# Attention's first two query blocks as one unit, and output rows turned with one PSUM bank at a time

## The chip, the cores and the metric

The kernel runs on one core of one Trainium2 chip. The metric is the device time of one execution in microseconds (us): lower is better. The kernel before takes 851.34 us, the median of three runs (850.49, 851.34, 851.52).

## What is computed

One layer of a hybrid encoder over 576 token columns: 512 of a prompt and 64 of a later chunk (the "sample"), model width 1024. One combined input projection feeds three groups of heads: a gated delta rule, a differential attention and a pooling mixer. Their outputs are concatenated, mapped back by `w_out`, added to the input, and a convolutional feed-forward network follows. The change touches the differential attention alone: 4 heads, each with two softmax maps of 64-dimensional keys, values of 128 dimensions, a block-causal mask and a norm for every head:

```python
def one_block(args):                      # prompt: blocks of 128 queries
    qi, bi = args
    q_chunk = (bi * Q_BLOCK + jnp.arange(Q_BLOCK)) // CHUNK
    mask = k_chunk[None, :] <= q_chunk[:, None]
    s = jnp.einsum('bqhmd,bkhmd->bhmqk', qi, k) * scale     # m: two maps
    s = jnp.where(mask, s, NEG_INF)
    p = jax.nn.softmax(s, axis=-1)
    w = p[:, :, 0] - lam * p[:, :, 1]
    return jnp.einsum('bhqk,bkhe->bqhe', w, v)
...
o_b = rmsnorm(o_b, b_norm) * (1.0 - lam_init)
```

Query block j (0 to 3) of the prompt sees key blocks 0 to j, so its two maps are 128 x 128(j+1).

## The kernel before

**Two streams on TensorE.** The large products (`gemm`, all through the helper `mm` at L85) form one long stream that `drive(projections())` walks. Every weight is split into a high and a low half (`w_hi`, `w_lo`) and so is every activation, and a product is three pairs of matmuls, 128 x 256 and 128 x 320 columns each, 576 in sum. Everything else (delta rule, attention, pooling) is written as generators that are put on a clock made of planned TensorE nanoseconds: `spawn(gen, delay)` starts one that many planned ns later, `yield N` puts its next piece N planned ns later, and `advance` issues what is due between two pairs of the stream. TensorE's order is the order in which this program issues matmuls; it is fixed at build time. The other engines' programs follow from it, and each runs its own in order.

**Banks.** Side work shares one pool of four PSUM banks (`psm`, tile name `m`, taken by `bank()`); the stream's results have two larger tiles of their own (`psg`, name `g`). In a row of the trace `m` is therefore a bank of the side work and `g` a result of the stream.

**One head of attention** (`attention()`, four heads one after the other). (1) `value_rows` turns the values with five transposes. (2) `scores_sample` fills two banks for the sample rows, and ScalarE takes the exponentials (L967, L968); `values_sample` needs one bank. (3) For j = 3, 2, 1, 0: `scores(a, j)` fills two banks with the maps; VectorE masks (L1005), takes maxima (L1006) and scales them (L1007); ScalarE takes the exponentials of both maps (L1010), which lets go of the banks; VectorE combines the maps into `p` (L1013 to L1016). Later `values(a, j)` takes a bank, transposes `p` into it (L1024, in the trace the helper's L89), ScalarE copies it out (L1026), the value matmuls write into the same bank, and VectorE copies the result into `oatt` (L1031); ScalarE sums its squares (L1033). At most three such units are in flight (`flight`). (4) When all five units of the head are done and the pooling groups too, `attn_out` computes the norm: VectorE L1040 to L1042, a reciprocal square root on GpSimd (L267), five scalings of `oatt` (L1047). After `yield 3500` it takes **two** banks at once, transposes the four prompt chunks into one and the sample chunk into the other, and ScalarE (L1055) and VectorE (L1056) write the high and low half of this head's rows of `mixed` (tile `wide`), 512 columns and then 64.

The attention of heads 1 to 3 overlaps the `w_out` products, whose order is the delta rule's and the pooling's inputs first, attention's last. Beside the attention VectorE also works for the stream: the low half of the weights (L175), of the pooling groups (L1149), the addition of the residual (L1159) and the low half of an early half-weight (L1095 in `own_weight`).

## Time and profile before

| | us |
|---|---|
| median of three runs | 851.34 |
| the profiled execution | 850.96 |
| its span, first to last instruction | 849.1 |
| TensorE busy in the span | 829.5 (98%) |
| VectorE busy | 536.0 (63%) |
| ScalarE busy | 359.9 (42%) |
| GpSimd busy | 109.5 (13%) |

1.9 us of the profiled execution lie outside its span. The attention runs from about 268 to about 400 us of the span. In the rows further down, a timeline row is: start, length in us, engine, line and operation, the tile written and the tiles read, shapes, how many instructions were joined (x), and in brackets how long the engine had been idle before it and who ended that idle time. Matmuls overlap at their ends, so the length of a joined row is longer than the distance from its start to the next row's start where nothing waits.

### The profile page before, as it was taken

Reading aid. Unit: us, or ns where it says so; the run is one execution under the profiler, and the core shown is the slowest. Engines: PE = TensorE matmul, PEld = TensorE weight load, DVE = VectorE, ACT = ScalarE, POOL = GpSimd, SP = SyncE. Lnnn points to the kernel's source line nnn. Section 1 sums busy time; section 2 is a strip of 40 time slices with the busy share of each in tenths; the row PEclk is TensorE's granted clock in tenths of the full one; section 3 lists DMA queues with packets and bytes.
Section 4 is the critical chain, followed back from the end, with each engine's and each line's share of the span. In section 5 each row is a group of like instructions: output and inputs, shape, how many; then the busy total and the mean of one; then the engine's idle time right before and its main releaser. Section 6 shows DMA issues by size and latency. Waiting matters only on the chain.

```text
span 849.1 us, 15939 instructions
## 1 busy us (share of the span) xinstructions
PE 829.5 (98%) x6342; PEld 803.9 (95%) x6342; DVE 536.0 (63%) x1203; ACT 359.9 (42%) x798; POOL 109.5 (13%) x166
## 2 busy tenths in 40 slices
PE   9989999999999999999999999999999999999996
PEld 8989999999999877789999999999999999999996
DVE  6798867881348667765767777776776773223423
ACT  7366661163444644543544444444434432222322
POOL 3132211220002000000011121121211210000001
PEclk9999999999999999999999999999999999999999
DMA  6242223242204323326622222222222223323313
GB/s 247 76 125 81 62 72 101 96 117 81 77 32 142 107 80 120 98 77 227 226 75 97 78 75 100 76 78 96 76 84 92 75 74 107 103 87 97 113 58 112
DMA packets 39032, 84.83 MB, mean 100 GB/s; under 512 B 9386, under 2 KB 14526, under 8 KB 38958
## 3 DMA queue, kind: packets, MB, share of 16 engines
q1 hardware_dynamic: 38014, 82.57, 30.1%
q10 hardware_dynamic: 944, 1.25, 0.4%
q8 instruction: 50, 0.82, 0.4%
q14 instruction: 24, 0.20, 0.1%
HBM read 72.98 MB, written 10.82 MB: 99 GB/s over the span
## 4 chain that ended last, share of the span: by engine, by line
PE 89%; DVE 4%; DMA 2%; ACT 2%; issue 1%; SPq 0%; POOLq 0%; POOL 0%; DVEq 0%; ACTq 0%
PE g L85 75%; PE m L85 11%; PE m L89 3%; DMA w_raw<-in_ffn_down_dram 1%; ACT w_hi L174 1%; DVE w_lo L175 1%; DMA x<-in_xT_dram 1%; DVE tmp L890 0%; DVE kq L596 0%; DMA w_raw<-in_w_out_dram 0%; ACT wide L348 0%; DVE oatt L1047 0%; DVE kq L601 0%; DVE p L1016 0%; DVE tmp L578 0%
## 5 line engine op out<-in xcount | busy, mean ns | idle before, releaser
L85 PE MATMUL g<-wide,w_hi 128*128 128x256 f32 x1472 | 265.6, 301 | 0.3
L85 PE MATMUL g<-t,w_hi 128*128 128x256 f32 (+1 forms) x1408 | 242.9, 294 | 0.0
L85 PEld LDWEIGHTS g<-wide,w_hi 128*128 128x128 f32 x1472 | 222.3, 190 | 2.9 <-DVE wide L349 0.6
L85 PEld LDWEIGHTS g<-t,w_hi 128*128 128x128 f32 x1408 | 210.2, 188 | 0.0
L174 ACT CAST w_hi<-w_raw 128x1024 fp32r<-128x1024 f32 (+2 forms) x109 | 110.9, 1017 | 172.8 <-PE g L85 161.8
L85 PE MATMUL g<-wide,w_lo 128*128 128x256 f32 x736 | 160.9, 300 | 0.5 <-DVE w_lo L175 0.5
L175 DVE TENSOR_TENSOR w_lo<-w_raw,w_hi 128x1024 fp32r<-128x1024 f32 (+2 forms) x109 | 128.2, 1176 | 49.9 <-ACT w_hi L174 48.9
L85 PE MATMUL g<-t,w_lo 128*128 128x256 f32 x704 | 150.2, 295 | 0.0
L85 PEld LDWEIGHTS g<-wide,w_lo 128*128 128x128 f32 x736 | 123.7, 190 | 2.5 <-issue 1.1
L85 PEld LDWEIGHTS g<-t,w_lo 128*128 128x128 f32 x704 | 117.4, 188 | 0.1
L1298 DVE SCALAR_TENSOR_TENSOR c<-u,par,c 128x511 f32<-128x511 f32 (+3 forms) x176 | 79.0, 512 | 2.5 <-ACT c L1294 2.5
L1301 POOL COPY fout<-u 128x4 f32<-128x4 f32 x44 | 51.2, 1163 | 223.1 <-DVE u L1292 223.1
L1292 DVE TENSOR_TENSOR u<-g,rstd 128x576 f32<-128x576 f32 x44 | 33.3, 758 | 59.7 <-PE g L85 58.2
L85 PE MATMUL g<-w,w_hi 128*128 128x256 f32 (+1 forms) x280 | 48.4, 295 | 0.0
L85 PEld LDWEIGHTS g<-w,w_hi 128*128 128x128 f32 x280 | 42.0, 188 | 0.0
L1294 ACT ACTIVATE c<-u,par 128x576 f32<-128x576 f32 x44 | 38.4, 873 | 4.6 <-DVE u L1292 1.8
L1318 ACT ACTIVATE s<-c 128x576 f32<-128x576 f32 x22 | 15.1, 688 | 45.8 <-DVE c L1300 45.8
L267 POOL TENSOR_TENSOR osc<-sso,mhalf 128x5 f32<-128x5 f32 x8 | 9.4, 1183 | 182.7 <-DVE sso L1042 77.9
L85 PE MATMUL g<-w,w_lo 128*128 128x256 f32 (+1 forms) x140 | 29.9, 294 | 0.0
L1203 ACT ACTIVATE junk<-m 128x128 f32<-128x128 f32 (+1 forms) x38 | 10.3, 274 | 40.2 <-PE m L89 32.2
L85 PE MATMUL g<-kq,w_hi 128*128 128x256 f32 (+1 forms) x128 | 25.0, 304 | 0.0
L1204 DVE TENSOR_TENSOR t<-m,nf 128x128 f32<-128x128 f32 (+1 forms) x38 | 10.6, 289 | 21.9 <-ACT junk L1203 21.9
(325 smaller groups left out, 1019.8 us busy)
## 6 DMA issues: line engine op xcount, KB each, us to landing
w_raw<-in_ffn_up_dram SPq DMA_DIRECT2D x44, 512.0 KB, 3.2
w_raw<-in_w_in_dram SPq DMA_DIRECT2D x30, 512.0 KB, 3.2
w_raw<-in_ffn_down_dram SPq DMA_DIRECT2D x16, 512.0 KB, 3.6
w_raw<-in_w_out_dram SPq DMA_DIRECT2D x8, 512.0 KB, 3.9
w_raw<-in_ffn_down_dram SPq DMA_DIRECT2D x8, 384.0 KB, 3.2
xr<-in_xT_dram SPq DMA_DIRECT2D x8, 288.0 KB, 3.2
x_d<-xr SPq DMA_DIRECT2D x8, 288.0 KB, 2.1
w<-x_d SPq DMA_DIRECT2D x8, 288.0 KB, 5.2
```

What stands on the lines that cost most here:

```text
L85: ordered(nc.tensor.matmul(out, lhsT=lhsT, rhs=rhs, start=start, stop=stop), n / 2.4 if rhs.dtype == F32R else max(54, n / 0.6))
L89: ordered(nc.tensor.transpose(out=out, in_=in_, identity=identity), 107)
L174: nc.scalar.copy(hi[:, :kt], raw)
L175: last_split[0] = nc.vector.tensor_sub(lo[:, :kt], raw, hi[:, :kt].bitcast(F32)).ins
L267: nc.gpsimd.tensor_tensor(out, x, epst[:x.shape[0], :x.shape[1]], op=ALU.pow)
L1203: nc.scalar.activation(junk[:n], src, AF.Square, scale=D ** -0.5, accum_out=op["part"][:n, c, m:m + 1])
L1204: nc.vector.tensor_mul(op["yt"][c][m // 4][:n, (m % 4) * P:(m % 4 + 1) * P], src, op["nf"][:n, m * P:(m + 1) * P])
L1292: nc.vector.tensor_mul(u, ps[:, O0:O1], rstd)
L1294: nc.scalar.activation(c, u, AF.Identity, scale=fw[:, 2, t:t + 1], bias=col("ffn_conv_b", t))
L1298: nc.vector.scalar_tensor_tensor(c[:, a + d:b], u[:, a:b - d], fw[:, j, t:t + 1], c[:, a + d:b], op0=ALU.mult, op1=ALU.add)
L1301: nc.gpsimd.tensor_copy(fout[:, :, :, t], u[:, NP - 64:].rearrange("p (s c) -> p s c", c=64)[:, :, 62:])
L1318: nc.scalar.activation(s, cv[0], AF.Silu)
```

## The change

`scores_low` and `values_low` replace the units j = 1 and j = 0 of each head by one unit. Its two banks hold block 1 in columns 0 to 255 and block 0 in columns 256 to 383. There is one mask per map for both blocks, still four maxima and four exponentials (these write their sums straight to where they are needed, so the copies of L1013 fall away), one reciprocal instead of two, still two combinations. `values_low` transposes three chunks into one bank, makes one copy of 128 x 384 on ScalarE, and after `yield 850` the three value matmuls and one copy of 128 x 256 on VectorE. The unit counts as one in `flight`; it is spawned with 5300, and the head goes on after 4500.

`attn_out` waits 4800 planned ns instead of 3500 (the last head still 3500) and takes one bank at a time: first the four prompt chunks, and then, after another `yield 2400` (heads 0 to 2), the sample chunk in a bank of its own. The number and the shapes of all matmuls and transposes stay, as do all DMAs.

```diff
@@ -1017,6 +1017,51 @@
                                                op0=ALU.mult, op1=ALU.add)
                 return pr[0]
 
+            def scores_low(a):
+
+                st = ap.tile([P, 3, 2], F32, name="statl", bufs=2)
+                maps = [bank()[:, :3 * P] for _ in range(2)]
+                blocks = ((1, slice(0, 2 * P)), (0, slice(2 * P, 3 * P)))
+                for j, cols in blocks:
+                    for m in range(2):
+                        r = slice(64 * m, 64 * m + 64)
+                        mm(maps[m][:, cols], a["qT"][r, j * P:(j + 1) * P], a["kT"][r, :(j + 1) * P])
+                for m in range(2):
+                    nc.vector.memset(maps[m].rearrange("p (b k) -> p b k", b=3)[:64, 1:, 64:], NEG)
+                    for j, cols in blocks:
+                        nc.vector.reduce_max(st[:, m, j:j + 1], maps[m][:, cols], axis=AX.X)
+                    nc.vector.tensor_mul(st[:, m], st[:, m], qneg[:, :2])
+                l1 = a["l1"][:, :2]
+                pr = [ap.tile([P, NP], F32, name=f"p{m}", bufs=3) for m in range(2)]
+                for m in range(2):
+                    for j, cols in blocks:
+                        total = l1[:, j:j + 1] if m == 0 else st[:, 2, j:j + 1]
+                        nc.scalar.activation(pr[m][:, cols], maps[m][:, cols], AF.Exp, scale=qscale[:, j:j + 1],
+                                             bias=st[:, m, j:j + 1], accum_out=total)
+                nc.vector.reciprocal(st[:, 2], st[:, 2])
+                nc.vector.scalar_tensor_tensor(st[:, 2], st[:, 2], nlam, l1, op0=ALU.mult, op1=ALU.mult)
+                for j, cols in blocks:
+                    nc.vector.scalar_tensor_tensor(pr[0][:, cols], pr[1][:, cols], st[:, 2, j:j + 1], pr[0][:, cols],
+                                                   op0=ALU.mult, op1=ALU.add)
+                return pr[0]
+
+            def values_low(a, pr):
+                pw = bank()
+                for c in range(3):
+                    transpose(pw[:, c * P:(c + 1) * P], pr[:, c * P:(c + 1) * P], ident)
+                wt = ap.tile([P, NP], F32, name="wt")
+                nc.scalar.copy(wt[:, :3 * P], pw[:, :3 * P])
+                yield 850
+                mm(pw[:, :P], wt[:, 2 * P:3 * P], a["v"][:, 0])
+                for c in range(2):
+                    mm(pw[:, P:2 * P], wt[:, c * P:(c + 1) * P], a["v"][:, c], start=c == 0, stop=c == 1)
+                nc.vector.tensor_copy(a["o"][:, :2], pw[:, :2 * P].rearrange("p (j d) -> p j d", j=2))
+                for j in range(2):
+                    junk = ap.tile([P, P], F32, name="junk")
+                    nc.scalar.activation(junk, a["o"][:, j], AF.Square, accum_out=a["ss"][:, j:j + 1])
+                a["left"] -= 2
+                flight[0] -= 1
+
             def values(a, j, pr):
                 nk = (j + 1) * P
                 pw = bank()
@@ -1045,16 +1090,20 @@
                 for c in range(5):
                     n = P if c < 4 else NS
                     nc.vector.tensor_scalar_mul(oatt[:n, c], oatt[:n, c], sc[:n, c:c + 1])
-                yield 3500
-                pp, p5 = bank(), bank()
-                for c in range(5):
-                    n = P if c < 4 else NS
-                    transpose(pp[:, c * P:(c + 1) * P] if c < 4 else p5[:, :n], oatt[:n, c], ident[:n, :n])
+                yield 3500 if h == HEADS - 1 else 4800
                 hi, lo = mixed[4 + h]
-                for ps, x, y in ((pp, 0, NP), (p5[:, :NS], NP, T)):
+                for chunks in (range(4), (4,)):
+                    pp = bank()
+                    for c in chunks:
+                        n = P if c < 4 else NS
+                        transpose(pp[:, c % 4 * P:c % 4 * P + n], oatt[:n, c], ident[:n, :n])
+                    x, y = (0, NP) if len(chunks) == 4 else (NP, T)
+                    ps = pp[:, :y - x]
                     nc.scalar.activation(hi[:, x:y], ps, AF.Identity, scale=bn_s)
                     nc.vector.scalar_tensor_tensor(lo[:, x:y], ps, bn_s, hi[:, x:y].bitcast(F32),
                                                    op0=ALU.mult, op1=ALU.subtract)
+                    if len(chunks) == 4 and h < HEADS - 1:
+                        yield 2400
                 done.add(f"out{h}")
 
             nxt = cached(0)
@@ -1078,11 +1127,15 @@
                 flight[0] += 1
                 spawn(values_sample(a, *scores_sample(a)), 6600)
                 yield 1500
-                for j in (3, 2, 1, 0):
+                for j in (3, 2):
                     yield from until(lambda: flight[0] < 3)
                     flight[0] += 1
                     spawn(values(a, j, scores(a, j)), 2800 + (j + 1) * 450)
                     yield 2700 + (j + 1) * 300
+                yield from until(lambda: flight[0] < 3)
+                flight[0] += 1
+                spawn(values_low(a, scores_low(a)), 5300)
+                yield 4500
                 spawn(attn_out(a), 0)
 
         zs, fs, pools = {}, {}, {}
```

How the program's order moves. In the rows below a name with a number is one tile, and the engines in brackets are those whose signals the instruction waits for.

TensorE, the low query blocks of head 1, before: block 0's maps (m_3972, m_3973), the transposes of block 1's `p` right behind, and the value matmuls of block 1.

```order
L85 MATMUL m_3972<-kq_2389 128x128 [waits PE_49]
L85 MATMUL m_3973<-kq_2389 128x128 [waits Activation_49]
L89 MATMUL m_3989<-cst_72,p0_3920 128x128 [waits DVE_49,Activation_49]
L89 MATMUL m_3989<-cst_72,p0_3920 128x128
L85 MATMUL g_3944<-kq_3359,w_hi_3774 128x256
L85 MATMUL g_3944<-kq_3359,w_hi_3774 128x320
L85 MATMUL g_3944<-kq_3359,w_lo_3775 128x256
L85 MATMUL g_3944<-kq_3359,w_lo_3775 128x320
L85 MATMUL g_3944<-kq_3402,w_hi_3774 128x256
L85 MATMUL g_3944<-kq_3402,w_hi_3774 128x320
L85 MATMUL m_3989<-v_out_3714,wt_3992 128x128 [waits Activation_49]
L85 MATMUL m_3989<-v_out_3714,wt_3992 128x128
```

The same place after: both blocks' maps in two banks (m_3876, m_3877), behind them the transposes of block 2's `p`, and then the sample chunk of head 0's output rows (oatt_3449, 128x64).

```order
L85 MATMUL m_3876<-kq_2389 128x256 [waits Activation_49]
L85 MATMUL m_3877<-kq_2389 128x256 [waits Activation_49]
L85 MATMUL m_3876<-kq_2389 128x128
L85 MATMUL m_3877<-kq_2389 128x128
L89 MATMUL m_3900<-cst_72,p0_3830 128x128 [waits DVE_49]
L89 MATMUL m_3900<-cst_72,p0_3830 128x128 x2
L89 MATMUL m_3906<-cst_72,oatt_3449 128x64 [waits DVE_49,PE_49]
L85 MATMUL g_3776<-wide_3533,w_hi_3534 128x256
L85 MATMUL g_3776<-wide_3533,w_hi_3534 128x320
L85 MATMUL g_3776<-wide_3532,w_lo_3535 128x256
L85 MATMUL g_3776<-wide_3532,w_lo_3535 128x320
L85 MATMUL g_3776<-wide_3532,w_hi_3534 128x256
```

Block 0's maps have moved up into block 1's banks, and the transposes behind them are block 2's; those of the low unit's `p` follow as three in a row, 5300 planned ns later. In this head an output transpose has moved in behind block 2's.

TensorE, head 2, before: block 3's maps (m_4110, m_4111), and the five output transposes of head 1 (oatt_3733) in two banks right behind.

```order
L85 MATMUL m_4110<-a_2787,a_2788 128x512 [waits DVE_49]
L85 MATMUL m_4111<-a_2787,a_2788 128x512 [waits DVE_49]
L89 MATMUL m_4127<-cst_72,oatt_3733 128x128 [waits PE_49,Activation_49]
L89 MATMUL m_4127<-cst_72,oatt_3733 128x128 [waits DVE_49] x3
L89 MATMUL m_4128<-cst_72,oatt_3733 128x64 [waits DVE_49,PE_49,Activation_49]
L85 MATMUL g_4096<-kq_3316,w_hi_3945 128x256
L85 MATMUL g_4096<-kq_3316,w_hi_3945 128x320
L85 MATMUL g_4096<-kq_3316,w_hi_3945 128x256
L85 MATMUL g_4096<-kq_3316,w_hi_3945 128x320
```

The same head after. The prompt chunks of head 1 (oatt_3700) were turned into m_4072 earlier, ahead of the sample unit's first products and behind block 3's maps; m_4085 is the sample unit's bank, m_4097 and m_4098 hold block 2's maps, m_4114 takes block 3's `p`.

```order
L85 MATMUL m_4085<-ew_4008,pr_4002 64x64
L85 MATMUL g_3942<-wide_3532,w_lo_3778 128x256
L85 MATMUL g_3942<-wide_3532,w_lo_3778 128x320
L85 MATMUL m_4097<-a_2787,a_2788 128x384 [waits Activation_49]
L85 MATMUL m_4098<-a_2787,a_2788 128x384 [waits Activation_49]
L89 MATMUL m_4114<-cst_72,p0_4046 128x128 [waits DVE_49,PE_49]
L89 MATMUL m_4114<-cst_72,p0_4046 128x128 x3
L89 MATMUL m_4121<-cst_72,oatt_3700 128x64 [waits Activation_49]
L85 MATMUL g_4129<-kq_3265,w_hi_3943 128x256
L85 MATMUL g_4129<-kq_3265,w_hi_3943 128x320
L85 MATMUL g_4129<-kq_3265,w_hi_3943 128x256
L85 MATMUL g_4129<-kq_3265,w_hi_3943 128x320
```

The sample chunk (m_4121) now stands behind block 3's transposes and ahead of the matmuls that finish m_4085 and m_4114. The same sequence stands in head 3 (m_4399).

VectorE at the same place, before: L1056 writes the low half of head 1's output rows between the maxima and the scale of block 3.

```order
L1005 MEMSET m_4110 64x64 [waits PE_49]
L1005 MEMSET m_4111 64x64 [waits PE_49]
L970 TENSOR_TENSOR mx_4071<-mx_4071 128x1 [waits Activation_49]
L1006 TENSOR_REDUCE stat_4109<-m_4110 128x1 [waits DVE_49]
L1006 TENSOR_REDUCE stat_4109<-m_4111 128x1 [waits DVE_49]
L971 RECIPROCAL mx_4071<-mx_4071 128x1 [waits DVE_49]
L1056 SCALAR_TENSOR_TENSOR wide_3533<-m_4127,bn_s_134,wide_3532 128x512 [waits Activation_49]
L1056 SCALAR_TENSOR_TENSOR wide_3533<-m_4128,bn_s_134,wide_3532 128x64 [waits Activation_49]
L1007 TENSOR_SCALAR stat_4109<-stat_4109,qneg_130 128x2 [waits DVE_49]
L972 TENSOR_TENSOR mx_4071<-mx_4071,coef_139 128x1 [waits DVE_49]
L974 TENSOR_SCALAR ew_4082<-cst_72,mx_4071 128x64 [waits DVE_49]
```

VectorE after: from block 3's combination to block 2's scale.

```order
L1015 SCALAR_TENSOR_TENSOR stat_4036<-stat_4036,lam_138 128x1 [waits DVE_49]
L1016 SCALAR_TENSOR_TENSOR p0_4046<-p1_4048,stat_4036,p0_4046 128x512 [waits DVE_49]
L1212 TENSOR_TENSOR xr_4125<-xr_4125,g_3942 128x576 [waits DMAHW7_49,DMAHW5_49,PE_49]
L1103 SCALAR_TENSOR_TENSOR wide_3533<-m_4072,bn_s_134,wide_3532 128x512 [waits Activation_49]
L1005 MEMSET m_4097 64x64 [waits PE_49]
L175 TENSOR_TENSOR w_lo_4131<-w_raw_3947,w_hi_4130 128x1024 [waits DMAHW6_49,Activation_49]
L1005 MEMSET m_4098 64x64 [waits PE_49]
L1006 TENSOR_REDUCE stat_4096<-m_4097 128x1 [waits DVE_49]
L1006 TENSOR_REDUCE stat_4096<-m_4098 128x1 [waits DVE_49]
L1007 TENSOR_SCALAR stat_4096<-stat_4096,qneg_130 128x2 [waits DVE_49]
```

The low half of the output rows (L1103 from m_4072) and the residual (L1212) now stand between block 3's `p` (L1016) and block 2's masks, and a weight split (L175) between the two masks. In head 3 the half-weight's low part (L1148, before L1095) now stands between L971 and L974, ahead of the sample's `ew`; before it stood behind L974.

VectorE, end of head 0 and start of head 1, before: the last pooling group's low half (L1149 from g_3723) stands ahead of head 0's norm.

```order
L1031 COPY oatt_3449<-m_3719 128x128 [waits PE_49]
L1149 SCALAR_TENSOR_TENSOR wide_3533<-g_3723,par_74,wide_3532 128x576 [waits Activation_49]
L1042 SCALAR_TENSOR_TENSOR sso_3451<-sso_3451,l1s_3450 128x5 [waits Activation_49]
L962 TENSOR_REDUCE mx_3744<-m_3738 128x1 [waits PE_49]
L963 TENSOR_REDUCE mx_3744<-m_3739 128x1 [waits PE_49]
L964 TENSOR_TENSOR mx_3744<-mx_3744 128x1 [waits DVE_49]
L965 TENSOR_TENSOR mx_3744<-mx_3744,qneg_130 128x1 [waits DVE_49]
L1159 TENSOR_TENSOR xr_3769<-xr_3769,g_3540 128x576 [waits DMAHW6_49,PE_49]
L1047 TENSOR_SCALAR oatt_3449<-oatt_3449,osc_3803 128x128 [waits Pool_49]
L1047 TENSOR_SCALAR oatt_3449<-oatt_3449,osc_3803 128x128 x3
```

After: L1202 is the same statement as L1149.

```order
L1087 SCALAR_TENSOR_TENSOR sso_3451<-sso_3451,l1s_3450 128x5 [waits Activation_49]
L970 TENSOR_TENSOR mx_3711<-mx_3711 128x1 [waits Activation_49]
L1005 MEMSET m_3743 64x64 [waits PE_49]
L971 RECIPROCAL mx_3711<-mx_3711 128x1 [waits DVE_49]
L1092 TENSOR_SCALAR oatt_3449<-oatt_3449,osc_3790 128x128 [waits Pool_49]
L1092 TENSOR_SCALAR oatt_3449<-oatt_3449,osc_3790 128x128
L1006 TENSOR_REDUCE stat_3742<-m_3743 128x1 [waits DVE_49]
L972 TENSOR_TENSOR mx_3711<-mx_3711,coef_139 128x1 [waits DVE_49]
L1092 TENSOR_SCALAR oatt_3449<-oatt_3449,osc_3790 128x128 x2
L1092 TENSOR_SCALAR oatt_3449<-oatt_3449,osc_3790 64x128
L1202 SCALAR_TENSOR_TENSOR wide_3533<-g_3736,par_74,wide_3532 128x576 [waits Activation_49]
```

The low half of the last pooling group (from g_3736) has moved behind the scaling of head 0's rows (L1092, before L1047) and behind block 3's first maximum. TensorE reads it after block 3's maps and four more pairs of the stream.

## Rows read from the trace of the kernel before

**Rows 1.** the page: engines, chain of the end, one group of instructions

```profile
PE 829.5 (98%) x6342; PEld 803.9 (95%) x6342; DVE 536.0 (63%) x1203; ACT 359.9 (42%) x798; POOL 109.5 (13%) x166
...
PE 89%; DVE 4%; DMA 2%; ACT 2%; issue 1%; SPq 0%; POOLq 0%; POOL 0%; DVEq 0%; ACTq 0%
...
L267 POOL TENSOR_TENSOR osc<-sso,mhalf 128x5 f32<-128x5 f32 x8 | 9.4, 1183 | 182.7 <-DVE sso L1042 77.9
```

**Rows 2.** windows: length, then each engine's busy us, granted clock, DMA share

```profile
410.00:700.00 290.00, 290.00 (x2203) 289.78 (x2202) 207.29 (x369) 122.06 (x142) 52.32 (x45) 1.00 0.27 88
...
830.00:850.00 20.00, 11.73 (x92) 11.27 (x91) 5.28 (x19) 5.03 (x15) 3.11 (x5) 0.92 0.34 119
```

**Rows 3.** timeline, TensorE in the attention, rows at its waits

```profile
309.61 0.86 PE L85 MATMUL m<-kq 64*128 64x384 f32 x2
311.13 0.91 PE L85 MATMUL m<-kq 64*128 64x384 f32 x2 [0.66 <-DVE wide L1056]
311.97 0.66 PE L89 MATMUL m<-cst,p 128*128 128x128 f32 x4
...
322.21 0.41 PE L89 MATMUL m<-cst,p 128*128 128x128 f32 x2 [0.67 <-DVE p L1016]
...
332.56 0.86 PE L89 MATMUL m<-cst,oatt 128*128 128x128 f32 x5 [0.94 <-ACT pr L967]
...
366.44 0.63 PE L89 MATMUL m<-cst,p 128*128 128x128 f32 x4 [1.03 <-DVE p L1016]
```

**Rows 4.** timeline, TensorE, bursts of maps that wait for nothing

```profile
289.14 0.70 PE L85 MATMUL m<-kq 64*128 64x256 f32 x4
289.77 0.55 PE L89 MATMUL m<-cst,p 128*128 128x128 f32 x3
...
293.61 0.49 PE L85 MATMUL m<-kq 64*128 64x128 f32 x4
294.03 0.44 PE L89 MATMUL m<-cst,p 128*128 128x128 f32 x2
...
337.81 0.92 PE L85 MATMUL m<-a 64*128 64x384 f32 x4
338.65 0.55 PE L89 MATMUL m<-cst,p 128*128 128x128 f32 x3
```

**Rows 5.** timeline, from VectorE's mask to ScalarE's first exponential, head 0, block 2

```profile
282.78 1.22 DVE L175 TENSOR_TENSOR w_lo<-w_raw,w_hi 128x1024 fp32r<-128x1024 f32 x1
...
284.73 0.11 DVE L1005 MEMSET m<- 64x64 f32 x1
...
287.02 0.19 ACT L1010 ACTIVATION_READ_ACCUMULATOR p<-m,stat,qscale 128x1 f32 x1
```

**Rows 6.** timeline, VectorE, head 1, block 3 up to the output rows' low half

```profile
302.70 0.76 DVE L1159 TENSOR_TENSOR xr<-xr,g 128x576 f32<-128x576 f32 x1 [0.41 <-PE g L85]
303.38 1.06 DVE L1047 TENSOR_SCALAR oatt<-oatt,osc 128x128 f32<-128x128 f32 x5
...
307.11 0.23 DVE L1007 TENSOR_SCALAR stat<-stat,qneg 128x2 f32<-128x2 f32 x1
...
310.33 0.75 DVE L1056 SCALAR_TENSOR_TENSOR wide<-m,bn_s,wide 128x512 fp32r<-128x512 f32 x1
```

**Rows 7.** timeline, TensorE and VectorE, last values of head 0, pairs, sample's `ew`

```profile
298.27 1.20 PE L85 MATMUL g<-xp,tmp 128*128 128x256 f32 x6
299.31 0.44 PE L85 MATMUL m<-v_out,wt 128*128 128x128 f32 x2
...
301.02 0.15 DVE L1042 SCALAR_TENSOR_TENSOR sso<-sso,l1s 128x5 f32<-128x5 f32 x1
...
306.92 0.69 PE L85 MATMUL g<-wide,w_hi 128*128 128x256 f32 x4
...
307.72 1.26 PE L85 MATMUL m<-ew,pr 128*128 128x64 f32 x10
```

**Rows 8.** timeline, ScalarE, head 3, cast of a half of w_out

```profile
362.90 0.62 ACT L1094 CAST a<-w_raw 128x512 fp32r<-128x512 f32 x1 [2.07 <-DMA w_raw<-in_w_out_dram]
```

## What the change does to the time: the prediction

> **What bounds the kernel now.** I read the page first, for the engine that sets the end: TensorE is busy 829.5 of 849.1 us and makes up 89% of the chain that ended last; VectorE has 4% of it [rows 1]. Then the windows, for where TensorE has slack: between 410 and 700 us it is busy 290.00 of 290.00 us at the full clock [rows 2]. So whatever the attention, which ends before 410 us, wins or loses on TensorE reaches the end undiminished, and whatever it wins on VectorE or ScalarE alone is worth nothing. Then TensorE's timeline through the attention, for its waits: there are seven, in four patterns [rows 3]. Last the bursts of the same shapes that wait for nothing [rows 4], since idle time alone underrates a wait: it also costs the overlap of two neighbouring bursts.
>
> All sums are made against the profiled execution, 850.96 us (849.1 us of span and 1.9 us around it). The median of 851.34 us is 0.4 us more, so I add my difference to the median.
>
> **What the change removes.** (a) Block 1's transposes stand right behind block 0's short maps and wait for `p`: 0.67 us idle. An undisturbed burst of that shape is 0.49 us long but hands over after 0.42 us (293.61 to 294.03) [rows 4], so each costs 0.74. The row in [rows 3] is one of three alike, 2.22 us in all. The unit is gone, and block 2's transposes, which now stand behind the low maps, wait for nothing in that place today (289.77) [rows 4]. (b) The output rows need two banks while the sample's exponentials still hold one: 0.94 us idle, twice [rows 3], with the overlap 2 x 1.01 = 2.02. One bank, taken 1300 planned ns later, is free by then. (c) In head 1 the output rows hold the bank that block 2's second map needs. The two maps run apart: 309.61 to 311.97 is 2.36 us [rows 3] where 337.81 to 338.65 is 0.84 [rows 4], so 1.52. (d) In head 3 block 3's transposes wait 1.03 us for `p` [rows 3], with the overlap 1.10; TensorE now arrives later, because it has waited before (4 below). Sum: 2.22 + 2.02 + 1.52 + 1.10 = 6.9 us.
>
> **What the merge itself saves.** The two bursts of low maps take 0.63 (289.14 to 289.77) and 0.42 us [rows 4]. Together they have 384 columns, and one burst of 384 takes 0.84 us [rows 4]: 0.21 us a head, 0.84 in all. The output rows, now in two pieces in three heads, break into the stream three times more, at about 0.1 us each (an estimate: the overlap of 0.07 above and a little). Net 0.5 us, between 0 and 0.8. VectorE's 7 and ScalarE's one instruction fewer a head count nothing by themselves. The matmuls stay, and no DMA is added; the value rows' stores only shift with their head.
>
> **What it adds: six waits.** They come from the order of instructions in the two places shown with the change and in head 3.
>
> 1. Head 0 to 1: VectorE writes the last pooling group's low half (L1202) behind the scaling of head 0's output rows, so behind the norm. From the end of the merged value matmuls: today 1.27 us pass from there to L1042 and 0.15 in it (299.31 + 0.44, then 301.02) [rows 7]; the wider copy and the second square add about 0.5; GpSimd's root 1.18 [rows 1]; five scalings 1.06 [rows 6]; a mask and maximum about 0.7 and the low half about 0.75 (as the 576-column row at 302.70) [rows 6]. That is 5.6, and some of it overlaps: 5.3. TensorE has to do meanwhile: six pairs at 0.267 (306.92 to 307.72 is three) [rows 7], a pooling group 1.04 (298.27 to 299.31) [rows 7], block 3's maps about 1.1: 3.8. Wait 1.5. Bounds: 0.8 and 1.9.
> 2. Head 1: the prompt's output rows take the sample bank, right behind the matmuls whose result VectorE has yet to copy out (L990). The nearest row is a short VectorE instruction, 0.23 us (307.11) [rows 6]; with its signals 0.4.
> 3. Head 2: block 3's transposes take the bank of the output rows, whose last reader is L1103, now behind `p` and the residual. From the end of block 3's maps: mask and maxima 1.6, the scalings 1.06, L1007 to the end of `p` 3.22 (307.11 to 310.33), the residual 0.68, the low half 0.75 [rows 6], in sum 7.3. TensorE has thirteen pairs (3.5), four transposes 0.4, the sample's products 1.2 [rows 7], block 2's maps 0.84 and the seams 0.2: 6.1. Wait 1.2, between 0.5 and 2.
> 4. Head 3: the sample's `ew` (L974) now stands behind the low part of a half of `w_out`, whose cast on ScalarE waits 2.07 us for its DMA today [rows 8]. Today `ew` is written ahead of it. Between 0, if the half has landed, and 2.1; I take 1.4, two thirds of today's wait for the half, since some of it runs out while TensorE works off the pairs ahead of these products.
> 5. Head 2: the sample chunk of the output rows (m_4121) finds all four banks taken: the sample's, block 3's and block 2's two maps. The first two are finished only by matmuls that stand behind it on TensorE, so it has to take a map's, once its exponentials are done. From the mask to the end of the first exponentials is 2.48 us (284.73 to 287.02 + 0.19) [rows 5]. A weight split stands between the two masks now, 1.14 to 1.22 more (282.78) [rows 5]. Four transposes of 0.4 lie beside it, and a signal: wait 3.1. Queued behind m_4121 is the whole stream.
> 6. Head 3: the same without the split: 2.48 - 0.4 = 2.1. In head 1 the same chunk stands behind the low unit's maps and finds the prompt chunk's bank long free: 0.
>
> With about 0.2 for seams the sum is 1.5 + 0.4 + 1.2 + 1.4 + 3.1 + 2.1 + 0.2 = 9.9 us. Waits one after the other on TensorE may swallow each other (a late TensorE finds the next bank free); 4 and (d), 3 and 5 are already counted so.
>
> **Net:** -6.9 - 0.5 + 9.9 = **+2.5 us**: 853.5 for the profiled execution, 853.8 for the median.
>
> A rule that speaks against the merge: the low unit makes `p` of both blocks ready only after four maxima and four exponentials. The Trainium skill, Perfetto Trace Analysis, section "Optimizing Scalar/DVE Operations", says that where VectorE and ScalarE aren't saturated but cause bubbles on other engines, breaking instructions up may let work finish sooner; both are unsaturated here. By it the bubbles of (a) would stay in another place, and the sum would be +4.7, 856.0. My rows say less: the unit has 5300 planned ns where block 1 had 3700.
>
> **The rivals.**
> - *Same.* The places are right and the sizes aren't: a wait that TensorE has already spent is charged twice, or the half of `w_out` lands in time (4 is 0) and 1 is 0.8. Then +2.5 - 1.4 - 0.7 = +0.4, 851.7. For it: 4 hangs on a DMA. Against it: 5 and 6, over half of the sum, hang on nothing but VectorE's and ScalarE's durations.
> - *Faster.* The sample chunk finds a bank without waiting, because TensorE comes to it after the first map's exponentials. The second pause of 2400 planned ns is planned time, not the engines' own. It decides at 3.1 us more work for TensorE ahead of the chunk in head 2 and 2.1 in head 3. Then 5 and 6 vanish: +2.5 - 5.2 = -2.7, 848.6. Against it: the order puts four transposes (0.4 us) there, and TensorE's order is fixed.
> - *Much slower: the clock falls.* In the attention TensorE's longest idle time is 1.03 us [rows 3]; wait 5 would be three times that. The only stretch with a clock below 1.00 is the last 20 us, 0.92, where TensorE is busy 11.73 us [rows 2]; by that row a fall costs 0.08 x 20 = 1.6 us. Then 853.8 + 1.6 = 855.4. The Trainium skill, TensorE: Matmul & The Clock Gate, section "HAM oscillation — how this bites in real kernels", describes gaps in the matmuls after which the engine starts again at the slow level; the trace shows none after waits of 1 us.
> - *The change does not do what it says:* an old wait stays, say (b) because the bank is still held, +2.0, 855.8. The longer pause speaks against it.
>
> **How the numbers follow.** A measurement of this kernel can tell about 0.2% (1.7 us) from no change: faster is below 849.6, slower above 853.0. The forecast has 0.63, same 0.20, faster 0.05, the clock 0.05, an old wait that stays 0.07. The unknown costs (1 by -0.7 and +0.4, 3 by -0.7 and +0.8, 4 by -1.4 and +0.7, the merge by +0.5 and -0.3) make the forecast's own range 852.4 to 855.6 if not all err one way. To hold 8 in 10 it goes down into the first rival and up to an old wait: 851.9 to 856.0. Faster 0.05; same 0.22, with a little of the forecast's lower end; slower 0.73.
>
> **What would show it.** Right: TensorE's waits in the profile after name VectorE's L1202 once, L1103 once, L974 once and twice a transpose of `oatt` 128x64 behind block 3's transposes, waiting 2 to 3 us for the exponentials of block 2; the waits for L1016 behind the short maps, for L967 and for L1056 are gone; TensorE's busy time falls by no more than 1 us; the clock stays at 1.00 from 270 to 400 us; after 410 us nothing changes but the start. Wrong: the `oatt` 128x64 rows without a wait (then it is faster), waits for `p` behind the merged maps, or idle time after 410 us that takes up a loss.

## The result and the profile after

The changed kernel takes 861.57 us, the median of four runs (861.02, 862.11, 862.2, 855.85), beside 851.43 us of four runs of the kernel before: a ratio of 1.0101, 95% interval 1.0077 to 1.0125, so 8.6 us slower by that ratio and 10.1 by the medians. I had forecast +2.5 us, and a range up to 856.0. The sign was right, the size was a quarter of the real one.

The profiled execution took 861.02 us, 859.2 in its span. The page's engine line and chain, as [rows 1]:

```profile
PE 836.9 (97%) x6342; PEld 810.3 (94%) x6342; DVE 530.8 (62%) x1175; ACT 358.1 (42%) x794; POOL 109.6 (13%) x166
...
PE 90%; DVE 4%; ACT 2%; DMA 2%; issue 1%; SPq 0%; POOLq 0%; POOL 0%; DVEq 0%; ACTq 0%
```

The same 6342 matmuls now keep TensorE busy for 836.9 us instead of 829.5. The forecast said that this time would fall a little. A longer busy time for the same work is the first sign that the matmuls themselves became slower. TensorE's timeline through the attention, only the rows with idle time ahead of them (start, length, what, idle time and who ended it), as [rows 3]:

```profile
304.65 0.53 PE L85 MATMUL g<-wide,w_hi 128*128 128x256 f32 x2 [1.41 <-DVE wide L1202]
...
312.39 0.66 PE L89 MATMUL m<-cst,oatt 128*128 128x128 f32 x4 [0.45 <-DVE oatt L990]
...
335.36 1.09 PE L89 MATMUL m<-cst,p 128*128 128x128 f32 x4 [1.31 <-DVE m L1005]
...
338.54 0.36 PE L89 MATMUL m<-cst,oatt 64*128 64x64 f32 x1 [2.09 <-ACT p L1010]
...
361.61 1.48 PE L85 MATMUL m<-ew,pr 128*128 128x64 f32 x10 [1.34 <-DVE l1s L1013]
...
368.06 0.36 PE L89 MATMUL m<-cst,oatt 64*128 64x64 f32 x1 [1.56 <-ACT p L1010]
```

These are the six waits of the prediction, in their places, and no others; all seven of [rows 3] are gone. The releaser named in two rows is an instruction that ended about 0.1 us after the real one (L1103 in head 2, L974 in head 3, by the order). But look at the lengths: four transposes of 128x128 are 1.09 us long at 335.36 and were 0.63 at 366.44 in [rows 3]. The windows say why (TensorE's busy us stands second, the granted clock third from the end):

```profile
320.00:330.00 10.00, 10.00 (x68) 7.93 (x67) 7.25 (x26) 3.38 (x10) 1.17 (x1) 1.00 0.47 143
330.00:340.00 10.00, 6.59 (x38) 5.00 (x37) 6.96 (x21) 5.73 (x14) 0.00 (x0) 0.77 0.31 108
340.00:350.00 10.00, 10.00 (x71) 9.09 (x71) 3.78 (x17) 3.67 (x15) 0.00 (x0) 0.89 0.02 7
350.00:360.00 10.00, 10.00 (x71) 8.03 (x69) 7.49 (x26) 4.26 (x12) 1.17 (x1) 1.00 0.36 112
360.00:370.00 10.00, 7.09 (x30) 4.56 (x29) 5.49 (x18) 4.64 (x13) 0.00 (x0) 0.63 0.19 56
370.00:380.00 10.00, 10.00 (x58) 8.83 (x57) 3.66 (x12) 3.43 (x11) 0.00 (x0) 0.69 0.02 7
```

TensorE's clock fell to its lower level (1.2 GHz) twice. Two finer windows, laid around the low stretches, show how much TensorE did in them:

```profile
335.20:342.10 6.90, 4.65 (x18) 3.56 (x19) 3.69 (x12) 2.21 (x6) 0.00 (x0) 0.51 0.46 163
362.70:376.10 13.40, 11.84 (x43) 8.61 (x45) 3.89 (x13) 3.50 (x12) 0.00 (x0) 0.50 0.06 25
```

16.49 us of work at half clock take 8.2 us longer. Some of that lies beside waits that get shorter for it (in a later run at full clock wait 5 is 2.56 us and wait 6 2.02; here they are 2.09 and 1.56), so about 7.3 us are the clock's, an estimate from these numbers. Another 0.4 us lie ahead of the attention: a short fall near the start, which the profile of the kernel before doesn't have (more on it at the end), moves the same transposes back, in the kernel before and after:

```profile
263.18 0.80 PE L89 MATMUL m<-cst,U 128*128 128x128 f32 x5
...
263.60 0.80 PE L89 MATMUL m<-cst,U 128*128 128x128 f32 x5
```

The rest of the 10.1, some 2.4 us, is the waits': TensorE's idle time (span less busy time) went from 19.6 to 22.3 us. After the attention nothing is taken back: between 410 and 700 us TensorE is busy 290.00 of 290.00 us, as in [rows 2].

```profile
410.00:700.00 290.00, 290.00 (x2204) 289.78 (x2203) 208.83 (x368) 123.61 (x147) 49.90 (x43) 1.00 0.29 99
```

### The profile page after: what moved, and what is told of

It is laid out like the page before. It is cut to its first block, busy times and chain, and to the rows that moved or that the text cites. A ratio compares the mean times of both kernels' runs of the same rounds, so it can differ in the third digit from the quotient of the medians.

```text
span 859.2 us, 15897 instructions
## 1 busy us (share of the span) xinstructions
PE 836.9 (97%) x6342; PEld 810.3 (94%) x6342; DVE 530.8 (62%) x1175; ACT 358.1 (42%) x794; POOL 109.6 (13%) x166
## 3 DMA queue, kind: packets, MB, share of 16 engines
q10 hardware_dynamic: 944, 1.25, 0.4%
## 4 chain that ended last, share of the span: by engine, by line
PE 90%; DVE 4%; ACT 2%; DMA 2%; issue 1%; SPq 0%; POOLq 0%; POOL 0%; DVEq 0%; ACTq 0%
PE g L85 75%; PE m L85 12%; PE m L89 3%; DMA w_raw<-in_ffn_down_dram 1%; DMA x<-in_xT_dram 1%; ACT w_hi L174 1%; DVE stat L1006 0%; DVE tmp L890 0%; DVE w_lo L175 0%; DMA w_raw<-in_w_out_dram 0%; ACT p L1010 0%; DVE kq L596 0%; ACT wide L348 0%; DVE oatt L1092 0%; DVE wide L1103 0%
## 5 line engine op out<-in xcount | busy, mean ns | idle before, releaser
L175 DVE TENSOR_TENSOR w_lo<-w_raw,w_hi 128x1024 fp32r<-128x1024 f32 (+2 forms) x109 | 128.2, 1176 | 50.6 <-ACT w_hi L174 49.6
```

The lines of the kernel that those rows point to most:

```text
L175: last_split[0] = nc.vector.tensor_sub(lo[:, :kt], raw, hi[:, :kt].bitcast(F32)).ins
```

## The experiments

**Theory 1:** the pairs of waits in heads 2 and 3 (3 with 5, 4 with 6) take the clock down, and the low clock is most of the loss. **Theory 2:** the clock falls for another reason, such as the load of the other engines, and the waits cost their idle time only. **Theory 3:** the first wait of each pair alone is enough. All ratios below are against the kernel before on the same chip.

**The second pause twice as long** (`e1_pause_4800`):

```diff
-                        yield 2400
+                        yield 4800
```

> The changed kernel with one number changed: the pause between the prompt part and the sample part of the output rows is 4800 instead of 2400, so that the sample chunk stands behind the matmuls that finish the sample unit and block 3, and finds a bank free. The waits in front of block 3's transposes in head 2 (1.31 us) and in front of the sample's products in head 3 (1.34 us) stay. Theory 1 (the second waits of heads 2 and 3, 2.09 and 1.56 us, keep TensorE's clock at 1.2 GHz and the low clock is 8 of the 10 us lost): 848.5 to 851.5 us, granted clock at least 0.97 from 330 to 390 us. Theory 2 (the loss is not of these waits; the clock falls for another reason, and only the idle time goes): 856 to 858.5 us with the clock still down between 330 and 380 us. Theory 3 (the first wait of each pair alone takes the clock down): falls that begin at the same places and are shorter, 852 to 856 us.

851.51 us, ratio 0.9994 (0.9982 to 1.0006). Its waits, and windows of 2 us around the one fall that is left:

```profile
335.19 1.06 PE L89 MATMUL m<-cst,p 128*128 128x128 f32 x4 [1.32 <-DVE m L1005]
...
358.79 1.33 PE L85 MATMUL m<-ew,pr 128*128 128x64 f32 x10 [1.29 <-DVE l1s L1013]
```

```profile
334.00:336.00 2.00, 0.81 (x5) 0.84 (x5) 2.00 (x4) 0.36 (x2) 0.00 (x0) 0.81 0.38 142
336.00:338.00 2.00, 2.00 (x10) 1.72 (x9) 1.48 (x5) 1.02 (x2) 0.00 (x0) 0.50 0.32 101
338.00:340.00 2.00, 2.00 (x14) 1.66 (x13) 0.28 (x1) 1.24 (x6) 0.00 (x0) 0.84 0.83 309
340.00:342.00 2.00, 2.00 (x15) 1.63 (x15) 1.43 (x6) 0.74 (x5) 0.00 (x0) 1.00 0.02 8
```

The sample chunk finds a bank free, waits 5 and 6 are gone, 3 and 4 stay as they were. The time lies at the upper edge of what theory 1 expected. One number of the change is worth the whole 10 us, although the two waits together were only 3.65 us idle. Theory 2 as written (856 to 858.5) falls. Theory 3 holds in part: after wait 3 the clock falls even so, but is back after some 3 us; after wait 4, of the same length, it doesn't fall at all (clock 1.00 from 360 to 390).

**No second pause** (`e4_no_pause`), the sample chunk right behind the prompt chunks:

```diff
-                    if len(chunks) == 4 and h < HEADS - 1:
+                    if False:
```

> The changed kernel without the pause between the two parts of the output rows: one bank for the prompt chunks, a second right behind for the sample chunk. Theory 1: both wait pairs of heads 2 and 3 go (block 3's transposes no longer stand behind the sample chunk's bank), smaller waits of 0.5 to 1 us come; 849 to 851.5 us, clock at 1.00 through the attention. Theory 2: 856 us or more.

850.67 us, ratio 0.9981 (0.9968 to 0.9995). Its longest waits in heads 2 and 3 are 0.46 and 0.82 us, and the clock stays at 1.00 from 270 to 410 us. Beside the merged unit, turning with one bank at a time is no loss in itself; the place of the sample chunk is.

**Each half of the change alone.** The merge with the old output rows (`e2_merge_only`), and the new output rows with the old two units (`e3_turn_only`); the hunks of the change that are undone:

```diff
-                yield 3500 if h == HEADS - 1 else 4800
...
+                yield 3500
+                pp, p5 = bank(), bank()
```

```diff
-                for j in (3, 2):
...
-                spawn(values_low(a, scores_low(a)), 5300)
-                yield 4500
+                for j in (3, 2, 1, 0):
```

> Half of the change: the low blocks as one unit, the output rows turned as before (two banks at once, after a pause of 3500). Theory 1: the merge by itself is good for the 2.2 us of waits behind the short maps and the 0.5 us of shorter bursts, and the output rows make one wait of about 2 us in head 1 and one of 1 to 1.5 in head 3; 849.5 to 852.5 us, clock at 1.00 or one short fall. Rival (the merged unit's later combination is what starves TensorE and brings the clock down): 855 us or more, waits for L1044.

> The other half: the output rows with one bank at a time and the pauses of the change (4800, 2400), the low blocks as two units as before. Theory 1: the sample chunk gets no second wait behind block 3's transposes, because the four units a head are in other places; one wait of about 2 us in head 1, and the waits for L1016 stay; 852 to 855 us without a fall of the clock. Rival (turning with one bank at a time is itself the cause): 857 us or more, with waits of 1.5 us and more in front of a transpose of oatt 128x64 in heads 2 and 3.

The merge alone: 852.54 us, ratio 1.0003 (0.9988 to 1.0018). The turning alone: 856.75 us, ratio 1.0045 (1.0028 to 1.0063). I had this last at 852 to 855 without a fall of the clock; it has six waits of 0.93 to 1.88 us in heads 1 to 3, five of them in front of transposes of `p`, and one fall. The merge alone lies at the upper end of its forecast; wait 1, the first row below, was not in it. The rows with idle time of the merge alone, and its windows after the second of them:

```profile
304.81 0.54 PE L85 MATMUL g<-wide,w_hi 128*128 128x256 f32 x2 [1.41 <-DVE wide L1198]
...
312.74 1.03 PE L89 MATMUL m<-cst,oatt 128*128 128x128 f32 x5 [2.01 <-ACT p L1010]
...
358.00 1.03 PE L89 MATMUL m<-cst,oatt 128*128 128x128 f32 x5 [1.14 <-DVE oatt L1092]
```

```profile
312.00:314.00 2.00, 1.26 (x7) 0.91 (x8) 0.72 (x4) 1.83 (x5) 0.00 (x0) 0.79 0.04 15
314.00:316.00 2.00, 2.00 (x10) 1.54 (x8) 1.29 (x3) 0.40 (x2) 0.00 (x0) 0.50 0.00 0
316.00:318.00 2.00, 2.00 (x11) 1.80 (x9) 0.28 (x1) 0.40 (x2) 0.00 (x0) 0.50 0.00 0
318.00:320.00 2.00, 2.00 (x10) 1.72 (x10) 0.29 (x1) 0.40 (x2) 0.00 (x0) 0.50 0.00 0
```

Wait 1 (L1198 is the pooling group's low half here) belongs to the merge with the old pauses, not to the output rows: the turning alone doesn't have it. No row waits for the merged unit's combination (L1044). And one wait of 2.01 us, with no second one behind it, brings a fall of more than 6 us.

**The waits filled instead of removed** (`e5_fill`). The order of the attention stays; transposes of a constant, into a tile that nobody reads, stand in front of the four waits of heads 2 and 3:

```diff
+            def fill(n):
+                pf = psg.tile([P, 1024], F32, name="g")
+                for _ in range(n):
+                    tc.keep_in_program_order(nc.tensor.transpose(out=pf[:, :P], in_=ident, identity=ident))
...
+                if j == 3 and a["h"] == 2:
+                    fill(12)
...
+                if a["h"] == 3:
+                    fill(12)
...
+                    if len(chunks) == 1 and h in (1, 2):
+                        fill(30 if h == 1 else 20)
```

> The changed kernel, its order of attention untouched, with transposes of a constant put in front of the four waits of heads 2 and 3 (12 in front of block 3's transposes in head 2, 30 in front of the sample chunk there; 12 in front of the sample's products in head 3, 20 in front of the sample chunk there), into a tile that nobody reads. TensorE waits for the same signals and is busy instead of idle meanwhile. Theory 1 (the idle time takes the clock down, and the low clock is 7 to 8 of the 10 us): clock 1.00 from 330 to 390 us, 853 to 856 us, although the work has become more. Theory 2 (the clock falls for another reason, such as the load of the other engines there): clock still down, 859 us or more.

855.83 us, ratio 1.0037 (1.0016 to 1.0059). TensorE does 74 transposes more than the changed kernel, waits for the same signals, and is about 5.7 us faster (861.57 to 855.83):

```profile
330.00:360.00 30.00, 30.00 (x227) 26.06 (x227) 19.18 (x62) 14.70 (x42) 1.17 (x1) 1.00 0.23 77
360.00:390.00 30.00, 29.90 (x225) 27.41 (x224) 16.39 (x49) 12.40 (x38) 1.17 (x1) 1.00 0.29 91
```

This is the run that settles it. The clock is at 1.00 where it fell before, with VectorE and ScalarE doing the same: it is TensorE's idle time that takes it down. And 3.2 us (0.0037 of 852; interval 1.4 to 5.0; 4.3 by the medians) is about what the change costs without these falls. Two of the ten executions, 858.31 and 858.52 us, have a lower mean clock (0.991) than the other eight (0.994 to 0.998), so some falls come even so; where they lie, no kept trace shows.

**Only the first wait of each pair filled, only the second** (`e6_fill_first`, `e7_fill_second`): the same helper with only its first two calls, or only its last.

> The changed kernel with 12 transposes of a constant only in front of the first wait of each pair (block 3's transposes in head 2, the sample's products in head 3); the second waits, of the sample chunk for a bank, stay idle (about 2.9 and 2.1 us). If the first wait is what takes the clock down and the second only prolongs it: clock at 1.00 or short falls of 3 to 4 us, 855 to 858 us. If the second wait by itself is enough: falls that begin after it, 858 us or more.

> The changed kernel with transposes of a constant only in front of the second wait of each pair (30 in head 2, 20 in head 3); the first waits stay idle (about 1.3 us each). As in the run with the longer second pause, the first wait alone should be followed by a short fall in some executions: 855.5 to 858 us. If a second, busy stretch doesn't bring the clock back, falls as long as in the changed kernel and 860 us or more.

856.32 us, ratio 1.0053 (1.0036 to 1.0070), and 856.72 us, ratio 1.0054 (1.0037 to 1.0071). The second waits left idle, with the windows beside them:

```profile
338.15 0.27 PE L89 MATMUL m<-cst,oatt 64*128 64x64 f32 x1 [2.56 <-ACT p L1012]
...
364.71 0.29 PE L89 MATMUL m<-cst,oatt 64*128 64x64 f32 x1 [2.02 <-ACT p L1012]
```

```profile
330.00:360.00 30.00, 27.44 (x204) 23.40 (x202) 19.53 (x65) 15.58 (x45) 1.17 (x1) 1.00 0.27 79
360.00:390.00 30.00, 27.98 (x196) 25.35 (x196) 15.70 (x46) 11.44 (x34) 1.17 (x1) 0.94 0.27 86
```

To fill either half of the pairs is nearly as good as to fill both. With the first waits filled, 2.56 us of idle time was followed by no fall and 2.02 by a short one; with the second filled, 1.32 was followed by a short one and 1.46 by none. A window of 30 us at 0.94 is 3.6 us at half clock, at most 1.8 us lost. With either half filled the kernel is about 5 us faster than the change (861.57 to 856.32 and 856.72): that part of the loss needs both waits of a pair. How the second wait does it shows in head 3, where both together make the fall of 13.4 us. Head 2's fall of 6.9 us is no longer than the one behind the single wait of the merge alone.

**Probes in a full stretch** (`p1_probe`, `p2_probe`), in the kernel before, in the up-projection of the feed-forward network: a transpose, k copies on ScalarE, a transpose that needs them.

```diff
+        def probe(k):
+            pb = bank()
+            transpose(pb[:, :P], ident, ident)
+            d = fp.tile([P, P], F32, name="probe")
+            for _ in range(k):
+                nc.scalar.copy(d, pb[:, :P])
+            pc = bank()
+            transpose(pc[:, :P], d, ident)
```

> The kernel before with nine probes in the up-projection of the feed-forward network, where TensorE is otherwise full: a transpose, k copies on ScalarE (k = 1, 2, 3, 4, 6, 8, 10, and twice a pair: 4 and 4, 4 and 8, with some four pairs of matmuls between) and a transpose that waits for them. Waits of about 0.5 to 3.5 us. Theory 1: the clock stays at 1.00 after waits up to 1 us, falls to 0.5 for 3 to 7 us after some of 1.3 us and more, and stays down longer where a second wait follows. Theory 2: the clock shows no relation with the waits. Theory 3 (length alone decides): a sharp length from which every wait is followed by a fall.

> As the run before, with the sizes in another order and later in the loop (k = pair 4 and 8, pair 4 and 4, 8, 6, 5, 4, 3, 2, and 3 three times), to see the same lengths at other moments. Theory 1: waits of 1.3 to 2 us are followed by a fall in some places and not in others; theory 3: the same length as in the run before decides.

882.04 and 885.6 us, one execution each. Three waits of the first, and the windows after them:

```profile
567.46 0.33 PE L89 MATMUL m<-cst,probe 128*128 128x128 f32 x1 [1.84 <-ACT probe L1274]
...
597.46 0.33 PE L89 MATMUL m<-cst,probe 128*128 128x128 f32 x1 [2.43 <-ACT probe L1274]
...
689.35 0.47 PE L89 MATMUL m<-cst,probe 128*128 128x128 f32 x1 [2.93 <-ACT probe L1274]
```

```profile
568.00:572.00 4.00, 4.00 (x21) 4.00 (x20) 1.08 (x2) 0.68 (x1) 0.00 (x0) 0.57 0.07 26
...
600.00:604.00 4.00, 4.00 (x33) 4.00 (x32) 1.62 (x2) 1.89 (x2) 0.80 (x1) 1.00 0.00 0
...
688.00:692.00 4.00, 2.65 (x11) 2.65 (x12) 0.44 (x1) 1.17 (x5) 0.00 (x0) 0.50 0.00 0
692.00:696.00 4.00, 4.00 (x22) 4.00 (x22) 0.10 (x1) 0.43 (x1) 0.00 (x0) 0.66 0.01 4
```

Over both runs: six single waits of 0.35 to 1.39 us, no fall; seven of 1.69, 1.84, 1.99, 2.28, 2.43, 2.88 and 3.03, a fall with all but 1.69, 1.99 and 2.43; five groups of two or three waits, a fall in all but one (1.69 and 1.30). So the length of one wait does not decide (2.43 without, 1.84 with a fall), and the strict theory 3 of these two runs, length alone, falls. Whether the waits of a group add up is not shown: in three of the four groups with a fall one wait is 1.90 us or longer and might have done it alone. The window at 688, low before the second wait of its pair (1.25 and 2.93 us) is over, is the changed kernel's head 3 in small: the fall lasts into the second window, some 6.7 us, twice as long as the others.

**The changed kernel once more** (`c1_changed_again`), unaltered, on another chip.

> The changed kernel once more, unaltered, for how its executions are spread. If each pair of waits brings the clock down in some executions only, the times fall into groups: about 856 us (no long fall), 858 (the one of head 2, some 2 us), 861 to 862 (both). If the clock's falls were a property of the chip of the first runs, this chip gives 855 to 857 throughout.

860.64 us (860.9, 860.38, 861.63, 857.23), ratio 1.0088 (1.0063 to 1.0112). Of the eight executions in the two sets six lie at 860.4 to 862.2 and two at 855.9 and 857.2, and these two have the highest mean granted clock, 0.992 and 0.994 beside 0.983 to 0.987; the group at 858 that I expected is empty. In the profiled one wait 5 is 2.56 us, since the clock falls only after it: a shorter fall in head 2, a longer wait, and the same time.

**Later output rows** (`b1_later`), and the same pauses without the merge (`b3_later_units`):

```diff
-                yield 3500 if h == HEADS - 1 else 4800
+                yield 3500 if h == HEADS - 1 else 8000
...
-                        yield 2400
+                        yield 4800
...
-                spawn(values_low(a, scores_low(a)), 5300)
+                spawn(values_low(a, scores_low(a)), 6500)
```

> The change with three other numbers: first pause before the output rows 8000 instead of 4800, second 4800 instead of 2400, the merged unit's delay 6500 instead of 5300. By the order of its instructions none of the six waits of the changed kernel stays, and two new ones of about half a us come (block 3's transposes for p in heads 1 and 2). Theory 1: the old 6.9 us and the merge's 0.5 are won, about 1 us is lost: 845.5 to 848 us, clock at 1.00 through the attention. Rival (what the attention wins is taken back by later waits, or the clock): 850 us or more.

> The fastest order so far without the merge: output rows with one bank at a time after pauses of 8000 and 4800, the low blocks as two units as before. What the merge itself is worth at this place: by the terms of the prediction 2.2 us of waits behind the short maps and 0.5 us of bursts. So 849 to 850.5 us, with waits for L1016 left; if the merge is worth nothing, 846 to 847.

846.5 us, ratio 0.9929 (0.9902 to 0.9956), and 849.31 us, ratio 0.9960 (0.9945 to 0.9976). The first is the fastest kernel of this study, 5 us faster than the kernel before and 15 faster than the change. All that is left of its waits in the attention, and its windows:

```profile
308.72 0.63 PE L89 MATMUL m<-cst,p 128*128 128x128 f32 x4 [0.42 <-DVE m L1005]
...
333.17 0.63 PE L89 MATMUL m<-cst,p 128*128 128x128 f32 x4 [0.60 <-DVE m L1005]
```

```profile
300.00:330.00 30.00, 29.57 (x210) 24.80 (x209) 22.14 (x77) 16.44 (x52) 2.33 (x2) 1.00 0.29 92
330.00:360.00 30.00, 29.40 (x207) 24.07 (x207) 20.81 (x69) 15.58 (x48) 1.17 (x1) 1.00 0.29 94
```

The difference of the two ratios, 0.0031 of 852 or 2.6 us, is what the merge is worth at this place; the intervals overlap, and the sets ran on two chips, so this is not exact. The waits for L1016 that it takes away are there again in the second (1.00 and twice 0.73 us).

## Why the prediction was wrong

**What bounds the kernel:** right. Every us that TensorE won or lost in the attention reached the end.

**The removed waits, 6.9 us:** right. None is left after the change, and the merge with later output rows wins 5 us.

**The merge, 2.2 + 0.5 us:** the two last runs agree with it (2.6, but by intervals that overlap). The Trainium skill, Perfetto Trace Analysis, section "Optimizing Scalar/DVE Operations", says that breaking up instructions may let work finish sooner where unsaturated VectorE and ScalarE cause bubbles on other engines. The bubbles that I drew from it for the merge didn't come: no run with the merged unit waits for its combination.

**The six waits:** right in place and nearly in size.

| wait | forecast, us | measured, us |
|---|---|---|
| 1, pooling group's low half | 1.5 | 1.41 |
| 2, sample bank | 0.4 | 0.45 |
| 3, block 3 in head 2 | 1.2 | 1.31 |
| 4, sample's `ew` in head 3 | 1.4 | 1.34 |
| 5, sample chunk in head 2 | 3.1 | 2.56 at full clock (2.09 at half) |
| 6, sample chunk in head 3 | 2.1 | 2.02 at full clock (1.56 at half) |

Two sums of the forecast don't come out as written, without bearing on the outcome: the terms of wait 5, 2.48 + 1.14 - 0.4, make 3.2 and not 3.1, and the unknown costs, added as squares, give 852.1 to 855.0 and not 852.4 to 855.6.

The size of wait 4 is in part luck. I had put the low part of a half-weight (L1148) ahead of `ew` and taken two thirds of its cast's wait. In the trace the cast's wait for its DMA is 1.39 us, and the low half of the output rows (L1103), which I had not counted there, stands ahead of `ew` as well:

```profile
359.88 0.69 DVE L1148 TENSOR_TENSOR a<-w_raw,a 128x512 fp32r<-128x512 f32 x1 [0.41 <-ACT a L1147]
...
360.56 0.74 DVE L1103 SCALAR_TENSOR_TENSOR wide<-m,bn_s,wide 128x512 fp32r<-128x512 f32 x1
361.22 0.25 DVE L974 TENSOR_SCALAR ew<-cst,mx 128x64 f32<-128x64 f32 x1
```

**The net, +2.5 us:** as a sum of idle time it holds: 2.7 more in the profile's span, and 3.2 by the times with all four late waits filled (1.4 to 5.0).

**The step that failed is the rival "the clock falls"**, in its price and in its chance. The price, 1.6 us a fall, came from the row 830 to 850 of [rows 2]: 0.92 over 20 us. That mean hid what was in it. In windows of 4 us of the same trace:

```profile
838.00:842.00 4.00, 3.62 (x29) 3.27 (x28) 0.96 (x3) 0.78 (x2) 0.24 (x1) 1.00 0.85 283
842.00:846.00 4.00, 0.11 (x1) 0.00 (x0) 1.97 (x7) 1.81 (x6) 1.10 (x2) 1.00 0.31 116
846.00:850.00 4.00, 0.00 (x0) 0.00 (x0) 0.00 (x0) 0.00 (x0) 0.00 (x0) 0.58 0.39 146
```

That fall lies where TensorE does nothing any more. It cost nothing, and says nothing on how long a fall lasts in the middle of work. Where TensorE works, the low stretches were 6.9 and 13.4 us long, and there were two of them, where I had counted one. The time that a fall costs is half of the work in it, 8.2 us for the 16.49 us of both, where the forecast's rival had 1.6. The chance, 0.05, rested on wait 5 alone ("three times" the longest wait of [rows 3]). My own sum had put 1.2 and 3.1 us, and 1.4 and 2.1 us, three to seven us apart, in one head each. I added them as idle time and never asked what two of them together do. The longest wait of the attention, 1.03 us idle at full clock, was a quarter of such a pair. And the trace of the kernel before had a longer one outside the attention, which I passed over: 2.71 us near the start, with the clock at 1.00 behind it. The changed kernel has the same wait there, 2.71 us again, and falls. The wait and the window behind it, before, and then the same window after:

```profile
52.26 1.00 PE L89 MATMUL m<-cst,kq 128*128 128x128 f32 x5 [2.71 <-DVE kq L601]
52.00:56.00 4.00, 3.73 (x28) 3.49 (x29) 3.94 (x17) 3.93 (x22) 1.26 (x4) 1.00 0.68 187
...
52.00:56.00 4.00, 3.75 (x18) 3.75 (x19) 3.94 (x17) 3.46 (x20) 1.26 (x4) 0.57 0.70 185
```

So one trace without a fall could not have told me that none would come; it would rather have kept the chance low. An unpriced cost of that kind belongs in the range: +2.5 and the two falls as measured would have been the upper end, some 860.

## What to carry to other kernels

When a change makes a saturated TensorE wait, sum its waits by place and not only in total: two of 1 to 3 us a few us apart can cost more than their idle time, as here, where the work after them ran at half clock. Take the price of a clock fall from a stretch in which TensorE works, in windows short enough to show 0.50: half of the work in it; a mean over a long window tells neither. And a step that needs a resource whose holders finish behind it in the same in-order queue has to be moved behind those holders: here one number, the second pause, was worth 10 us.

## What the runs showed of the hardware

The clock went down after single waits of 1.3 us (at 335 us, the changed kernel) and stayed up after one of 2.56 us (the run with the first waits filled), in the same head; executions of the changed kernel differ by 5 to 6 us, the faster ones at the higher mean clock. In the probes, between full stretches, a fall lasted 3 to 4 us, or some 6.7 where a second wait ran into it; behind the wait of 2.01 us of the merge alone, with side work between the pairs, more than 6; with a second wait inside it, in head 3 of the changed kernel, 13.4. The Trainium skill, TensorE: Matmul & The Clock Gate, section "A second HAM failure mode: psum-queue depth-cycling", tells of short idle times between groups of matmuls, while PSUM banks are cycled through, that make the clock swing between its two levels. The trace agrees for three of the four late waits, which are for banks (the fourth is for `ew`): the clock at 1.00 and 0.50 in turn, and no fall there with the same waits filled.

A fall also comes near the start, where the programs agree: the clock is 0.57 from 52 to 56 us in the changed kernel's profile and 1.00 in that of the kernel before, though TensorE is busy 1.55 of the 4 us ahead of it in both. The same wait in the same code is followed by a fall in one execution and by none in another. The kernel before differs between executions too, from 850.31 to 857.92 us over all its runs beside the experiments, the slowest at a mean clock of 0.987. The one fall seen near the start is worth 0.4 us, so it doesn't explain that; with one kept trace of that kernel the cause stays open.
